# Attention: the heads' norm taken from the unnormalised result, with epsilon scaled by the squared sum of exponentials

## The chip, the cores and the metric

One core of one Trainium2 chip. The metric is the device time of one launch in microseconds (us); a kernel's time is the median of its runs. A difference of about 0.2% (7.6 us) is the least that a measurement of this kernel can tell from none.

## The reference, cut to what matters

The program is two layers of a diffusion backbone over 1024 latent tokens, with 256 context tokens that share the weights (in the second layer the context is only read). Each layer: a norm, an input projection, three parallel mixers (a long convolution, an mLSTM, differential attention), an output projection, and a mixture of 32 experts. The change lies in the attention alone:

```python
def diff_core(q, k, v, lam):
    s = jnp.einsum('bqhmd,bkhmd->bhmqk', q, k, preferred_element_type=jnp.float32) * (DA_HD ** -0.5)
    pr = jax.nn.softmax(s, axis=-1)
    a = pr[:, :, 0] - lam * pr[:, :, 1]
    return jnp.einsum('bhqk,bkhe->bqhe', a.astype(v.dtype), v)
...
    def finish(o):
        return (rmsnorm(o, p['da_subln_w']) * (1.0 - lam_init)).reshape(o.shape[0], o.shape[1], DA_V)
```

Four heads, each with two score maps (m = 0, 1) of 64 channels; the 128 output channels of a head are divided by their root mean square plus `NORM_EPS` = 1e-6. Write S0 and S1 for a row's sums of exponentials. The kernel never divides by S0: it forms u = e0 - (lam S0 / S1) e1 and U = u V, so that the head's output is U / S0, and the norm is (U / S0) / sqrt(mean(U^2) / S0^2 + eps). That equals U / sqrt(mean(U^2) + eps S0^2).

## The kernel before, in words

`attention` works through units. A unit is one head and 256 query tokens (16 per layer: four heads of four blocks); layer 0 has one more, the context tokens of all four heads. `x` = 0, 1 is the half of 128 query rows, `m` the score map. A pass of the loop runs three units at once, each one stage further: unit i gets its scores, maxima and exponentials, unit i-1 is transposed and rounded, unit i-2 is multiplied with V and its norm begun, and the last two steps of unit i-3's norm are done too. So a full pass is one with i from 3 to 15; the norm's last steps are missing in passes 0 to 2.

The order within a pass is written out by hand in `AT_ORDER` (L1240), and holds on PE, DVE, ACT and POOL (a manual schedule); SP's queue, which issues the loads of q, k and v and the stores, stands in an order that a planner set. The letters:

- `S`xm: six matmuls for one score tile `at_sc` (L1107, PE). There are two such tiles in PSUM.
- `M`xm: the negated row maximum (L1113, DVE). `E`xm: the exponentials and their sum (L1122, ACT).
- `C`x (`comb`): a reciprocal (L1130) and a product (L1131) that give c = -lam S0 / S1, then a reciprocal of S0 into `at_R` (L1132), all DVE on 128x1 tiles; on POOL the tile e1 is multiplied by c (L1134, 1280 columns) and added to e0 (L1138, 1280 columns, two inputs).
- `T`n: four transposes (L1150, PE); `U`n: the high part (L1161, ACT); `L`n: the low part (L1166, DVE).
- `O` and `Q` are steps of `out1`: `O` for unit i-2, `Q` for unit i-3. The first two `O` are 15 matmuls each with V (`at_av`, helper lines L68 to L70), the third copies and squares the result (ACT), the fourth sums the squares with ones (`at_st`, L1184, PE), the fifth does on DVE two products with `at_R` (L1188, L1189) and `mean + eps` (L186 in the helper `rstd`), and on POOL the power -1/2 (L188). In the next pass the first `Q` multiplies that by `at_R` (L1192, DVE), the second transposes it to a row vector `at_rb` (L1196, PE), the third scales the result (L1198, DVE) and stores it (L1199, SP).
- `W`: one sixteenth of the output projection's weights is loaded, and split on ACT (L1253) and POOL (L1254).

All of `at_t`, `at_av`, `at_st` and `at_rb` share two buffers in PSUM. While one of them holds the sums of `at_av`, the others take turns in the second: `at_rb` can be written only after `L1` has read its tile, and `T1` only after `L0`.

Of the kernel before, what the change touches and what calls it, by code (L numbers as in the profile page):

```python
# [8 lines left out]
F32 = mybir.dt.float32  # L9
# [3 lines left out]
OP = mybir.AluOpType  # L13
# [10 lines left out]
EPS = 1e-6  # L24
# [5 lines left out]
class Kern:  # L30
# [332 lines left out]
    def fft1(self, z, W, G, gD, pool, ps):  # L363
# [5 lines left out]
        for c in range(4):  # L369
            zn = [self.hsplit(pool, x(c + 1)) for x in z] if c < 3 else None  # L370
            S = pool.tile([128, 2, 2, 256], F32, name="f_s", bufs=2)
            for ri in range(2):
                p = ps.tile([128, 512], F32, name="f_p", tag="mm")
                for n, (w, x) in enumerate(zip(W, zz)):
                    self.mm3(p, [w[:, h, ri, :] for h in range(2)], x, start=(n == 0), stop=(n == len(W) - 1))
                nc.scalar.copy(S[:, ri].rearrange("p a b -> p (a b)"), p)
                self.qa.dma_start(rows[c, ri], S[:, ri].rearrange("p a b -> p (a b)"))
            zz = zn
# [246 lines left out]
    def hyena(self, l, cx, p, ps):  # L625
# [9 lines left out]
        for o in range(2):  # L635
# [28 lines left out]
            for c in range(4):  # L664
                S = p.tile([128, 2, 2, 256], F32, name="f_s", bufs=2)
                for ri in range(2):
# [369 lines left out]
    def attention(self, l, cx, p, pk, ps, psc, fill):  # L1036
        tc, nc, I = self.tc, self.nc, self.I
# [2 lines left out]
        N = len(pairs)  # L1040
        st = {}

        def prep(i):

            ctx = pairs[i] is None
            kt = lambda: pk.tile([128, 1280], F32R, name="at_k", bufs=6)
            vt = lambda: pk.tile([128, 10, 128], F32R, name="at_v", bufs=4)
            if ctx:
                kd = [[kt()[:, 0:1024].rearrange("p (h t) -> p h t", h=4) for y in range(2)] for m in range(2)]
                for m in range(2):  # L1050
                    for y in range(2):
                        for x in range(2):
                            nc.sync.dma_start(kd[m][y][64 * x:64 * x + 64].bitcast(F32),
                                              self.qkD[l][1, :, y, 64 * m:64 * m + 64, SEQ:].rearrange("h d t -> d h t"))
                v = [vt() for x in range(2)]
                for x in range(2):
                    for k in range(2):
                        nc.sync.dma_start(v[x][:, k:8:2, :].bitcast(F32),
                                          self.vD[l][x, SEQ + k * 128:SEQ + (k + 1) * 128, :]
                                          .rearrange("p (h e) -> p h e", h=4))  # L1060
                q = [kt()[:, 0:1024].rearrange("p (m h t) -> p m h t", m=2, h=4) for _ in range(2)]
                for qi in range(2):
                    for m in range(2):
                        c = SEQ + qi * 128
                        for y in range(2):
                            nc.sync.dma_start(q[qi][64 * y:64 * y + 64, m].bitcast(F32),
                                              self.qkD[l][0, :, y, 64 * m:64 * m + 64, c:c + 128]
                                              .rearrange("h d t -> d h t"))
            else:
                h, qb = pairs[i]  # L1070
                q = pk.tile([128, 2, 256], F32R, name="at_q", bufs=2)
                for y in range(2):
                    nc.sync.dma_start(q[64 * y:64 * y + 64].bitcast(F32), self.qkD[l][0, h, y, :, qb * 256:(qb + 1) * 256]
                                      .rearrange("(m d) t -> d m t", m=2))
                if qb == 0:
                    kd = [[kt() for y in range(2)] for m in range(2)]
                    for m in range(2):
                        for y in range(2):
                            for x in range(2):
                                nc.sync.dma_start(kd[m][y][64 * x:64 * x + 64, :].bitcast(F32),  # L1080
                                                  self.qkD[l][1, h, y, 64 * m:64 * m + 64])
                    v = [vt() for x in range(2)]
                    for x in range(2):
                        nc.sync.dma_start(v[x].bitcast(F32), self.vD[l][x].rearrange("(k p) e -> p k e", p=128)
                                          [:, :, h * 128:(h + 1) * 128])
                    st["kv"] = kd, v
                kd, v = st["kv"]
            nh = 4 if ctx else 1
            st[i] = dict(ctx=ctx, kd=kd, v=v, q=q, nh=nh, nk=8 if ctx else 10, E=[[None, None], [None, None]],
                         sc=[[None, None], [None, None]], t={},  # L1090
                         R=p.tile([128, 4, 2], F32, name="at_R", bufs=4),
                         S=[p.tile([128, 5, 4], F32, name=f"at_S{x}", bufs=2) for x in range(2)])

        def smm(i, x, m):
            u = st[i]
            w = u["nk"] * 128
            sc = u["sc"][x][m] = psc.tile([128, 1280], F32, name="at_sc", bufs=2)
            if u["ctx"]:
                for h in range(4):
                    for y in range(2):  # L1100
                        nc.tensor.matmul(sc[:, h * 256:(h + 1) * 256], u["q"][x][:, m, h, :], u["kd"][m][y][:, h, :],
                                         start=(y == 0), stop=(y == 1))
            else:
                for c in range(0, w, 512):
                    n = min(512, w - c)
                    for y in range(2):
                        nc.tensor.matmul(sc[:, c:c + n], u["q"][:, m, x * 128:(x + 1) * 128],  # L1107
                                         u["kd"][m][y][:, c:c + n], start=(y == 0), stop=(y == 1))

        def smx(i, x, m):  # L1110
            u = st[i]
            w, sc = u["nk"] * 128, u["sc"][x][m]
            nc.vector.tensor_reduce(u["S"][x][:, m, 0:u["nh"]], sc[:, 0:w].rearrange("p (h t) -> p h t", h=u["nh"]),  # L1113
                                    axis=AX.X, op=OP.max, negate=True)

        def sexp(i, x, m):
            u = st[i]
            w, S, g = u["nk"] * 128, u["S"][x], u["nk"] * 128 // u["nh"]
            e = u["E"][x][m] = p.tile([128, 1280], F32, name=f"at_e{m}", bufs=2 if m else 4)[:, 0:w]
            for h in range(u["nh"]):  # L1120
                cs = slice(h * g, (h + 1) * g)
                nc.scalar.activation(e[:, cs], u["sc"][x][m][:, cs], AF.Exp, bias=S[:, m, h:h + 1],  # L1122
                                     accum_out=S[:, 2 + m, h:h + 1])

        def comb(i, x):

            u = st[i]
            S, E, n = u["S"][x], u["E"][x], u["nh"]
            c = S[:, 4, 0:n]
            nc.vector.reciprocal(c, S[:, 3, 0:n])  # L1130
            nc.vector.scalar_tensor_tensor(c, S[:, 2, 0:n], nlam, c, op0=OP.mult, op1=OP.mult)  # L1131
            nc.vector.reciprocal(u["R"][:, 0:n, x], S[:, 2, 0:n])  # L1132
            if n == 1:
                nc.gpsimd.tensor_scalar(E[1], E[1], c, 1.0, op0=OP.mult, op1=OP.mult)  # L1134
            else:
                e = E[1].rearrange("p (h t) -> p h t", h=n)
                nc.gpsimd.tensor_tensor(e, e, c.unsqueeze(2).to_broadcast([128, n, 256]), op=OP.mult)
            nc.gpsimd.tensor_tensor(E[0], E[0], E[1], op=OP.add)  # L1138
# [29 lines left out]
        def out1(u, h, k0, nk):  # L1168
            o = ps.tile([128, 512], F32, name="at_av", tag="mm")
# [11 lines left out]
            R = u["R"][:, h if u["ctx"] else 0, :]  # L1181
            o = ps.tile([128, 512], F32, name="at_st", tag="mm")
# [1 line left out]
                nc.tensor.matmul(o[:, x:x + 1], sq[:, x * 128:(x + 1) * 128], self.ones[:, 0:1],  # L1184
                                 start=True, stop=True)
            yield
            t = p.tile([128, 2], F32, name="at_ms", bufs=2)
            nc.vector.tensor_tensor(t, o[:, 0:2], R, op=OP.mult)  # L1188
            nc.vector.tensor_tensor(t, t, R, op=OP.mult)  # L1189
            r = self.rstd(p, t, 2, 1.0 / 128)  # L1190
            yield
            nc.vector.tensor_tensor(R, r, R, op=OP.mult)  # L1192
            yield
            o = ps.tile([128, 512], F32, name="at_rb", tag="mm")
            for x in range(2):
                nc.tensor.transpose(o[:, x * 128:(x + 1) * 128], R[:, x:x + 1].to_broadcast([128, 128]), self.ident)  # L1196
            yield
            nc.vector.scalar_tensor_tensor(ob, ob, sub, o[:, 0:256], op0=OP.mult, op1=OP.mult)  # L1198
            nc.sync.dma_start(self.yTD[l][4 + h, :, u["qb"] * 256:(u["qb"] + 1) * 256], ob)  # L1199
# [7 lines left out]
        with tc.manual_schedule(engines={E_.PE, E_.DVE, E_.Activation, E_.Pool}):  # L1207
            for i in range(N + 3):
                prev, cur = cur, None
                if 0 <= i - 2 < N:  # L1210
                    u = st[i - 2]
# [20 lines left out]
            if cx:  # L1232
                for a in range(0, 4, 2):
# [3 lines left out]

    AT_ORDER = """S00 O M00 T0 S01 T1 U0 O L0 E00 Q Q U1 M01 S10 T2 L1 E01 T3 O Q S11 U2 C0 O T4 M10 U3 E10 L2 L3  # L1240
                  M11 U4 O E11 L4 C1 W"""


# [426 lines left out]
    S = 9  # L1670
# [194 lines left out]
    R = 5, 2, 2, 2, 1.5  # L1865
# [327 lines left out]
```

## Time and profile before

| | |
|---|---|
| median of 3 runs | 3781.49 us (3776.14 to 3783.82) |
| the profiled execution | 3769.79 us, its span 3768.0 us |
| busy share of the span | PE 85%, PE weight load 69%, DVE 73%, ACT 49%, POOL 46% |
| attention, layer 0 | from about 705 to 975 us of the span |
| attention, layer 1 | from about 2606 to 2832 us |
| mean granted PE clock | 0.927 of full speed |

PE is TensorE, PEld its weight loads, DVE VectorE, ACT ScalarE, POOL GpSimd, SP the queue that issues most transfers. Shares are means over stages with different limits, so the attention must be read by itself.

### The profile page before, as it was taken

The page shows a single profiled execution, that of the slowest core. Times are in us where ns is not written, and L with a number is a line of the kernel's source. Part 1 is how long each engine was busy: PE and PEld are TensorE (multiplying, and loading weights), DVE is VectorE, ACT ScalarE, POOL GpSimd, SP SyncE. Part 2 cuts the span into 40 slices and gives each one's busy share as a digit, 9 for nine tenths or more (in the row PEclk, how much of TensorE's full clock was granted, in tenths as well). Part 3 has the DMA queues.
Part 4 walks back from the last instruction along what each step waited for, and adds up shares of the span by engine and source line. Part 5 has one row for each costly group of instructions (what it writes and reads, how often), then busy time and mean ns, then how long its engine had stood idle before and what let it go on. Part 6 is the DMA issues. An engine that isn't in the chain of part 4 may idle for free. (4 is left out here: it accounts for less than half of the span.)

```text
span 3768.0 us, 49472 instructions
## 1 busy us (share of the span) xinstructions
PE 3211.9 (85%) x16750; PEld 2604.6 (69%) x16750; DVE 2751.6 (73%) x4303; ACT 1844.7 (49%) x2747; POOL 1714.6 (46%) x1293
## 2 busy tenths in 40 slices
PE   5999889787689889999996799987887988898893
PEld 2667778777577667777764777786776867676672
DVE  5444577588477798788776836875885788888887
ACT  3323333465332457577575324334663266666673
POOL 5001443376354345455553703343764355555555
PEclk7999999999799899999998899998998999999996
DMA  6889667443555679988886635766415588888885
GB/s 212 278 281 327 178 205 210 129 123 96 163 184 194 216 254 323 328 314 319 300 330 251 228 111 176 229 202 168 122 52 175 198 325 279 329 328 319 325 329 200
DMA packets 388513, 877.22 MB, mean 233 GB/s; under 512 B 60765, under 2 KB 244584, under 8 KB 332192
## 3 DMA queue, kind: packets, MB, share of 16 engines
q1 hardware_dynamic: 328945, 644.13, 51.4%
q10 hardware_dynamic: 25103, 145.74, 10.9%
q0 software_dynamic: 34208, 84.14, 6.9%
q8 instruction: 134, 2.20, 0.2%
q14 instruction: 123, 1.01, 0.1%
HBM read 750.32 MB, written 154.77 MB: 240 GB/s over the span
## 5 line engine op out<-in xcount | busy, mean ns | idle before, releaser
L1609 DVE TENSOR_TENSOR e_lo<-e_raw,e_hi 128x1024 fp32r<-128x1024 f32 x570 | 901.0, 1611 | 132.2 <-ACT e_hi L1608 124.9
L1608 ACT CAST e_hi<-e_raw 128x1024 fp32r<-128x1024 f32 x760 | 773.4, 1049 | 292.5 <-PE e_h L70 148.2
L1609 POOL TENSOR_TENSOR e_lo<-e_raw,e_hi 128x1024 fp32r<-128x1024 f32 x190 | 504.1, 2653 | 404.1 <-ACT e_hi L1608 352.7
L69 PE MATMUL e_h<-e_lo,e_xh 128*128 128x512 f32 x1024 | 422.8, 413 | 65.7 <-DVE e_lo L1609 53.0
L68 PE MATMUL e_h<-e_hi,e_xh 128*128 128x512 f32 x1024 | 413.3, 408 | 11.7 <-ACT e_hi L1608 8.9
L70 PE MATMUL e_h<-e_hi,e_xl 128*128 128x512 f32 x1024 | 405.6, 397 | 0.0
L69 PEld LDWEIGHTS e_h<-e_lo,e_xh 128*128 128x128 f32 x1024 | 195.5, 191 | 149.5 <-DVE e_lo L1609 83.6
L68 PE MATMUL p_u<-hT,u_w 128*128 128x512 f32 (+1 forms) x768 | 289.7, 377 | 3.6 <-ACT u_w L60 3.6
L69 PE MATMUL p_u<-hT,u_w 128*128 128x512 f32 (+1 forms) x768 | 287.3, 374 | 0.0
L70 PE MATMUL p_u<-hT,u_w 128*128 128x512 f32 (+1 forms) x768 | 285.6, 373 | 0.0
L68 PEld LDWEIGHTS e_h<-e_hi,e_xh 128*128 128x128 f32 x1024 | 195.2, 191 | 65.3 <-ACT e_hi L1608 24.4
L1122 ACT ACTIVATE at_e<-at_sc,at_S 128x1280 f32<-128x1280 f32 (+1 forms) x144 | 177.7, 1238 | 105.3 <-DVE at_S L1113 97.1
L1107 PE MATMUL at_sc<-at_k,at_q 128*128 128x512 f32 (+1 forms) x768 | 193.9, 389 | 32.3 <-DMA at_k<-qkD 23.6
L70 PEld LDWEIGHTS e_h<-e_hi,e_xl 128*128 128x128 f32 x1024 | 195.4, 191 | 36.5 <-issue 0.5
L69 PE MATMUL e_y<-e_lo,e_hh 128*128 128x512 f32 x512 | 205.5, 403 | 17.3 <-DVE e_lo L1609 14.2
L1113 DVE TENSOR_REDUCE at_S<-at_sc 128x1 f32<-128x1280 f32 (+1 forms) x132 | 194.2, 1472 | 35.1 <-PE at_sc L1107 29.9
L70 PE MATMUL e_y<-e_hi,e_hl 128*128 128x512 f32 x512 | 199.7, 397 | 7.1 <-DVE e_hl L61 7.1
L1138 POOL TENSOR_TENSOR at_e<-at_e,at_e 128x1280 f32<-128x1280 f32 (+1 forms) x66 | 192.2, 2913 | 5.5
L1134 POOL TENSOR_SCALAR at_e<-at_e,at_S 128x1280 f32<-128x1280 f32 x64 | 85.7, 1339 | 236.1 <-DVE at_R L1132 175.3
L1107 PEld LDWEIGHTS at_sc<-at_k,at_q 128*128 128x128 f32 x768 | 143.9, 202 | 62.1 <-issue 23.9
L68 PE MATMUL e_y<-e_hi,e_hh 128*128 128x512 f32 x512 | 175.2, 411 | 10.5 <-ACT e_hi L1608 6.6
L68 PEld LDWEIGHTS p_u<-hT,u_w 128*128 128x128 f32 x768 | 148.1, 193 | 35.8 <-issue 7.9
(574 smaller groups left out, 8195.4 us busy)
## 6 DMA issues: line engine op xcount, KB each, us to landing
e_raw<-in_moe_w_dram SPq DMA_DIRECT2D x259, 1024.0 KB
e_raw<-in_moe_w_dram ACTq DMA_DIRECT2D x121, 1024.0 KB
adaw<-in_ada_w_dram SPq DMA_DIRECT2D x48, 1024.0 KB
at_k<-qkD SPq DMA_DIRECT2D x64, 320.0 KB
u_raw<-in_w_in_dram SPq DMA_DIRECT2D x36, 512.0 KB
cb_y<-yD SPq DMA_DIRECT2D x36, 512.0 KB
hW<-in_c_hw_dram POOLq DMA_DIRECT2D x32, 512.0 KB, 4.6
at_v<-vD SPq DMA_DIRECT2D x16, 640.0 KB
```

The source lines that it names most:

```text
L68: mm(out, L[0], R[0], start=start, stop=False)
L69: mm(out, L[0], R[1], start=False, stop=False)
L70: mm(out, L[1], R[0], start=False, stop=stop)
L1107: nc.tensor.matmul(sc[:, c:c + n], u["q"][:, m, x * 128:(x + 1) * 128], u["kd"][m][y][:, c:c + n], start=(y == 0), stop=(y == 1))
L1113: nc.vector.tensor_reduce(u["S"][x][:, m, 0:u["nh"]], sc[:, 0:w].rearrange("p (h t) -> p h t", h=u["nh"]), axis=AX.X, op=OP.max, negate=True)
L1122: nc.scalar.activation(e[:, cs], u["sc"][x][m][:, cs], AF.Exp, bias=S[:, m, h:h + 1], accum_out=S[:, 2 + m, h:h + 1])
L1134: nc.gpsimd.tensor_scalar(E[1], E[1], c, 1.0, op0=OP.mult, op1=OP.mult)
L1138: nc.gpsimd.tensor_tensor(E[0], E[0], E[1], op=OP.add)
L1608: self.nc.scalar.copy(hi, raw)
L1609: (self.nc.gpsimd if pool else self.nc.vector).tensor_tensor(lo, raw, hi.bitcast(F32), op=OP.subtract)
```

## The change

The sum S0 of both halves is kept in one tile `at_S` (128x2x5x4). `comb` no longer takes 1/S0: after the second half one instruction writes eps S0^2 for both halves into `at_R`. In the norm one instruction forms mean(U^2) + eps S0^2, the power -1/2 follows on POOL, and its result goes to the transposes as it is. The step of `out1` that multiplied by `at_R` is gone, and one `Q` of `AT_ORDER` with it. (The loop over columns in `smm` is rewritten with the same bounds; a name there is set and not used.)

```diff
@@ prep
-                         S=[p.tile([128, 5, 4], F32, name=f"at_S{x}", bufs=2) for x in range(2)])
+                         S=p.tile([128, 2, 5, 4], F32, name="at_S", bufs=2))
@@ comb
             nc.vector.reciprocal(c, S[:, 3, 0:n])
             nc.vector.scalar_tensor_tensor(c, S[:, 2, 0:n], nlam, c, op0=OP.mult, op1=OP.mult)
-            nc.vector.reciprocal(u["R"][:, 0:n, x], S[:, 2, 0:n])
+            if x == 1:
+                s = u["S"][:, :, 2, 0:n].rearrange("p x h -> p h x")
+                nc.vector.scalar_tensor_tensor(u["R"][:, 0:n, :], s, EPS, s, op0=OP.mult, op1=OP.mult)
@@ out1
-            t = p.tile([128, 2], F32, name="at_ms", bufs=2)
-            nc.vector.tensor_tensor(t, o[:, 0:2], R, op=OP.mult)
-            nc.vector.tensor_tensor(t, t, R, op=OP.mult)
-            r = self.rstd(p, t, 2, 1.0 / 128)
-            yield
-            nc.vector.tensor_tensor(R, r, R, op=OP.mult)
+            t = p.tile([128, 2], F32, name="at_ms", bufs=3)
+            nc.vector.scalar_tensor_tensor(t, o[:, 0:2], 1.0 / 128, R, op0=OP.mult, op1=OP.add)
+            r = p.tile([128, 2], F32, name="rs_r", bufs=3)
+            nc.gpsimd.tensor_tensor(r, t, self.nhalf.to_broadcast([128, 2]), op=OP.pow)
             yield
             o = ps.tile([128, 512], F32, name="at_rb", tag="mm")
             for x in range(2):
-                nc.tensor.transpose(o[:, x * 128:(x + 1) * 128], R[:, x:x + 1].to_broadcast([128, 128]), self.ident)
+                nc.tensor.transpose(o[:, x * 128:(x + 1) * 128], r[:, x:x + 1].to_broadcast([128, 128]), self.ident)
@@ AT_ORDER
-    AT_ORDER = """S00 O M00 T0 S01 T1 U0 O L0 E00 Q Q U1 M01 S10 T2 L1 E01 T3 O Q S11 U2 C0 O T4 M10 U3 E10 L2 L3
+    AT_ORDER = """S00 O M00 T0 S01 T1 U0 O L0 E00 Q U1 M01 S10 T2 L1 E01 T3 O Q S11 U2 C0 O T4 M10 U3 E10 L2 L3
```

How this stands on DVE is shown for one full pass in two pieces. The first is the start of a pass, from the second half's c of the pass ahead (`C1`) to `L1`; before:

```order
L1130 RECIPROCAL at_S_6510<-at_S_6510 128x1
L1131 SCALAR_TENSOR_TENSOR at_S_6510<-at_S_6510,at_nl 128x1
L1132 RECIPROCAL at_R<-at_S_6510 128x1
L1113 TENSOR_REDUCE at_S_6651<-at_sc 128x1
L1166 TENSOR_TENSOR at_A_6678<-at_t,at_A_6677 128x4x128
L1192 TENSOR_TENSOR at_R<-rs_r,at_R 128x2
L1113 TENSOR_REDUCE at_S_6651<-at_sc 128x1
L1166 TENSOR_TENSOR at_A_6678<-at_t,at_A_6677 128x4x128
```

and now, in the same place:

```order
L1131 RECIPROCAL at_S<-at_S 128x1
L1132 SCALAR_TENSOR_TENSOR at_S<-at_S,at_nl 128x1
L1135 SCALAR_TENSOR_TENSOR at_R<-at_S 128x2
L1114 TENSOR_REDUCE at_S<-at_sc 128x1
L1169 TENSOR_TENSOR at_A_6668<-at_t,at_A_6667 128x4x128
L1114 TENSOR_REDUCE at_S<-at_sc 128x1
L1169 TENSOR_TENSOR at_A_6668<-at_t,at_A_6667 128x4x128
```

The product into `at_R` between `L0` and `M01` is gone, and a product of `at_S` with itself stands where the reciprocal stood. The second piece is the norm's fifth step, between `M11` and `L4`; before:

```order
L1113 TENSOR_REDUCE at_S_6652<-at_sc 128x1
L1188 TENSOR_TENSOR at_ms<-at_st,at_R 128x2
L1189 TENSOR_TENSOR at_ms<-at_ms,at_R 128x2
L186 TENSOR_SCALAR rs_v<-at_ms 128x2
L1166 TENSOR_TENSOR at_A_6678<-at_t,at_A_6677 128x512
```

and now:

```order
L1114 TENSOR_REDUCE at_S<-at_sc 128x1
L1191 SCALAR_TENSOR_TENSOR at_ms<-at_st,at_R 128x2
L1169 TENSOR_TENSOR at_A_6668<-at_t,at_A_6667 128x512
```

Three instructions became one. After the first half's c (`C0`) the reciprocal into `at_R` is gone with nothing in its place. In the whole program DVE has 3253 rows for 3393; on PE the order is the same row for row, with the transposes of `at_rb` reading `rs_r` for `at_R`. Outside the attention a few neighbours on ACT, POOL and SP change places, in the output projection and the experts; the loads of k and q on SP stand as before.

## Rows read from the trace of the kernel before

**Rows 1.** Busy time by stretch: length, PE, PEld, DVE, ACT, POOL, granted clock, DMA, GB/s.

```profile
770.58:784.86 14.28, 11.78 (x82) 10.40 (x81) 12.64 (x22) 9.47 (x17) 10.48 (x6) 1.00 0.50 139
801.17:805.17 4.00, 2.42 (x19) 2.22 (x19) 4.00 (x4) 1.42 (x3) 3.73 (x2) 1.00 0.00 0
805.17:809.17 4.00, 3.42 (x16) 3.12 (x17) 2.69 (x6) 2.40 (x5) 1.85 (x2) 0.68 0.32 97
...
729.17:740.99 11.82, 11.23 (x79) 10.06 (x78) 10.56 (x21) 9.47 (x17) 10.52 (x6) 1.00 0.15 44
```

**Rows 2.** Timeline of DVE in a full pass: start, length in us, instruction.

```profile
777.66 0.48 DVE L1198 SCALAR_TENSOR_TENSOR at_o<-at_o,at_sub,at_rb 128x256 f32<-128x256 f32 x1 [0.53 <-PE at_rb L1196]
...
784.65 0.22 DVE L1131 SCALAR_TENSOR_TENSOR at_S<-at_S,at_nl 128x1 f32<-128x1 f32 x1
784.79 0.16 DVE L1132 RECIPROCAL at_R<-at_S 128x1 f32<-128x1 f32 x1
...
786.29 0.69 DVE L1166 TENSOR_TENSOR at_A<-at_t,at_A 128x512 fp32r<-128x512 f32 x1
786.90 2.51 DVE L1192 TENSOR_TENSOR at_R<-rs_r,at_R 128x2 f32<-128x2 f32 x1
789.33 1.48 DVE L1113 TENSOR_REDUCE at_S<-at_sc 128x1 f32<-128x1280 f32 x1
790.74 0.67 DVE L1166 TENSOR_TENSOR at_A<-at_t,at_A 128x512 fp32r<-128x512 f32 x1
...
792.55 0.22 DVE L1131 SCALAR_TENSOR_TENSOR at_S<-at_S,at_nl 128x1 f32<-128x1 f32 x1
```

**Rows 3.** Timeline of POOL in the same pass.

```profile
785.04 1.34 POOL L1134 TENSOR_SCALAR at_e<-at_e,at_S 128x1280 f32<-128x1280 f32 x1 [0.88 <-DVE at_R L1132]
786.47 2.93 POOL L1138 TENSOR_TENSOR at_e<-at_e,at_e 128x1280 f32<-128x1280 f32 x1
789.36 1.26 POOL L1254 TENSOR_TENSOR wo<-wo_raw,wo 128x512 fp32r<-128x512 f32 x1
```

**Rows 4.** Instructions that touch at_R: count, shortest, median and longest in ns.

```profile
L1192 DVE TENSOR_TENSOR at_R<-rs_r,at_R x36: 149/2514/2573, 743.0 to 2831.3; 128x2 f32<-128x2 f32 x36
```

**Rows 5.** Timeline of PE in the same pass.

```profile
785.34 1.40 PE L1107 MATMUL at_sc<-at_k,at_q 128*128 128x512 f32 x6
787.04 0.66 PE L1150 MATMUL at_t<-cst,at_e 128*128 128x128 f32 x4 [0.30 <-DVE at_A L1166]
...
789.14 0.28 PE L70 MATMUL at_av<-at_A,at_v 128*128 128x256 f32 x1
791.46 0.43 PE L1196 MATMUL at_rb<-cst,at_R 128*128 128x128 f32 x2 [2.05 <-DVE at_A L1166]
```

**Rows 6.** Timelines of DVE and POOL in pass 2, ahead of the first L1192.

```profile
733.66 1.29 POOL L1254 TENSOR_TENSOR wo<-wo_raw,wo 128x512 fp32r<-128x512 f32 x1
734.38 0.59 DVE L1131 SCALAR_TENSOR_TENSOR at_S<-at_S,at_nl 128x1 f32<-128x1 f32 x1
736.57 2.93 POOL L1138 TENSOR_TENSOR at_e<-at_e,at_e 128x1280 f32<-128x1280 f32 x1
738.95 0.14 DVE L1188 TENSOR_TENSOR at_ms<-at_st,at_R 128x2 f32<-128x2 f32 x1
```

**Rows 7.** Timelines of DVE and PE where a head ends and the next begins.

```profile
865.47 0.48 DVE L1198 SCALAR_TENSOR_TENSOR at_o<-at_o,at_sub,at_rb 128x256 f32<-128x256 f32 x1 [0.53 <-PE at_rb L1196]
...
875.56 1.17 PE L1107 MATMUL at_sc<-at_k,at_q 128*128 128x512 f32 x5 [1.93 <-DMA at_k<-qkD]
877.12 1.48 DVE L1113 TENSOR_REDUCE at_S<-at_sc 128x1 f32<-128x1280 f32 x1
```

**Rows 8.** Timeline of DVE: two L1192 in a row, with a lower PE clock between.

```profile
801.17 2.52 DVE L1192 TENSOR_TENSOR at_R<-rs_r,at_R 128x2 f32<-128x2 f32 x1
816.52 2.52 DVE L1192 TENSOR_TENSOR at_R<-rs_r,at_R 128x2 f32<-128x2 f32 x1
```

**Rows 9.** Timeline of DVE in the context unit's last norm step.

```profile
973.99 0.16 DVE L1192 TENSOR_TENSOR at_R<-rs_r,at_R 128x2 f32<-128x2 f32 x1 [1.71 <-POOL rs_r L188]
```

More of the change, by code (lines that the diff above doesn't have):

```diff
@@ L1096, in smm @@
             w = u["nk"] * 128
+            c0 = m * 1280
             sc = u["sc"][x][m] = psc.tile([128, 1280], F32, name="at_sc", bufs=2)
@@ L1103, in smm @@
             else:
-                for c in range(0, w, 512):
-                    n = min(512, w - c)
+                for c, n in ((0, 512), (512, 512), (1024, 256)):
                     for y in range(2):
@@ L1112, in smx @@
             w, sc = u["nk"] * 128, u["sc"][x][m]
-            nc.vector.tensor_reduce(u["S"][x][:, m, 0:u["nh"]], sc[:, 0:w].rearrange("p (h t) -> p h t", h=u["nh"]),
+            nc.vector.tensor_reduce(u["S"][:, x, m, 0:u["nh"]], sc[:, 0:w].rearrange("p (h t) -> p h t", h=u["nh"]),
                                     axis=AX.X, op=OP.max, negate=True)
@@ L1117, in sexp @@
             u = st[i]
-            w, S, g = u["nk"] * 128, u["S"][x], u["nk"] * 128 // u["nh"]
+            w, S, g = u["nk"] * 128, u["S"][:, x], u["nk"] * 128 // u["nh"]
             e = u["E"][x][m] = p.tile([128, 1280], F32, name=f"at_e{m}", bufs=2 if m else 4)[:, 0:w]
@@ L1127, in comb @@
             u = st[i]
-            S, E, n = u["S"][x], u["E"][x], u["nh"]
+            S, E, n = u["S"][:, x], u["E"][x], u["nh"]
             c = S[:, 4, 0:n]
```

## The prediction

> **What bounds the attention now.** I read the shares first, stretch by stretch; then DVE's timeline through one pass, since DVE is the busiest engine there beside PE; then POOL's and PE's over the same microseconds. A full pass, from one `M00` to the next, takes 14.28 us; DVE works 12.64 of it, PE 11.78, POOL 10.48, ACT 9.47 [rows 1]. Neither is full, so the question is what each waits for.
>
> DVE's timeline answers it. Of its 12.64 us one instruction of 128x2 elements takes 2.51: L1192, the product into `at_R` [rows 2]. Over both layers its 36 instances have a median of 2514 ns and a shortest of 149 [rows 4], so it does not work for 2.4 us, it is held. By what: it starts at 786.90 and ends at 789.41; POOL's sum over 1280 columns starts at 786.47 and ends at 789.40 [rows 2, 3]. The two ends agree to 0.01 us. L1192 reads both inputs from SBUF. So does L1131, and where POOL works in the same way L1131 takes 0.59 us for its usual 0.22, ending with POOL's L1254 (734.97 and 734.95) [rows 2, 6]. L1188 has one input in PSUM, and takes 0.14 in the midst of POOL's sum [rows 6]. So on these rows a DVE instruction with two inputs in SBUF waits out POOL's two-input instruction, and one with an input in PSUM does not.
>
> Who waits for L1192: DVE is in order, so `M01` begins at 789.33 and `L1` ends at 791.41 [rows 2]. `at_rb` needs the buffer that `L1` empties, and starts at 791.46, though the matmuls ahead of it on PE had issued their last at 789.14, about 0.11 before the next could go: PE stands still from 789.25, 2.21 us [rows 5]. Behind `at_rb` in PE's queue stand `S10` and all the rest of the pass.
>
> The trace holds a control. Pass 2 runs everything but the norm's last steps, and takes 11.82 us [rows 1].
>
> **The change part by part.** The sum is made against the profiled execution, 3769.79 us for a span of 3768.0; the median of the runs is 11.7 us (0.3%) above it, and I carry the difference over to the median.
>
> *L1192 goes.* DVE can start `M01` at 786.90 instead of 789.33, 2.43 us earlier, if its scores are there: `S01` ends at 786.74 [rows 5]. `L1` would end near 789.0, and then not `L1` but PE decides: `at_rb` at 789.25 in place of 791.46. Gain 2.21 us a pass. What is late next is PE itself. The power whose result `at_rb` now reads directly is computed between `C0`'s and `C1`'s work on POOL, a third of a pass before.
>
> *At `C1`* a product of `at_S` with itself takes the place of the reciprocal. Its kind cost 0.22 us in L1131, the reciprocal 0.16 [rows 2]: 0.06 lost ahead of `M00`. Bounds: nothing, and 0.4 if it is held as L1131 was in pass 2 [rows 6]. I take 0.06, since no POOL work is under way at that point in rows 3: L1134 starts only at 785.04. Net 2.15 us a pass, 12.13 in place of 14.28. The control agrees: 11.82 plus the slot of `at_rb` and the scaling behind it.
>
> *The other small instructions* of a pass (the reciprocal at `C0`, two of the three in the norm's fifth step) are some 0.1 to 0.2 us each. I take nothing for them in a full pass: after `C0` DVE waits for `S10`, and after `L4` for the exponentials of `E11`. If that cover is gone they are worth up to 0.4 a pass.
>
> *A wait that grows.* POOL's L1254 follows `C1`'s sum and ends at 790.62 [rows 3]. In the shorter pass `C0`'s L1131, 1.09 us behind `at_rb` (792.55 against 791.46 [rows 2, 5]), comes at 790.34 and is held until 790.62, as in pass 2. `M10`, queued behind it, needs `S10`, which ends about 1.6 us after `at_rb` starts, at 790.85. So it costs nothing; at worst 0.37 a pass (0.59 less 0.22).
>
> *Where a head begins* (passes 4, 8, 12) half of its keys arrive late. `S01` then resumes 10.09 us after the scaling L1198 of the pass ahead (875.56 against 865.47), while `M01` starts at 877.12, right behind the held L1192: today the wait costs nothing [rows 7]. In an ordinary pass `S01` starts 7.68 us after L1198 (785.34 against 777.66) [rows 2, 5]. So L1192 was the cover of that transfer. Its loads are issued behind the store that L1198 feeds, so they come earlier only as L1198 does. With L1192 gone, `M01` waits for the scores, to 876.73 plus a hand-over: 0.3 us gained. I take 0.25. Bounds 0 and the full 2.15.
>
> *The clock.* In pass 7 PE is granted 0.68 of full speed for some microseconds, a mean of its two levels of 1.2 and 2.4 GHz, right after a stretch in which it was busy for only 2.42 of 4 us [rows 1]. That pass takes 15.35 us (801.17 to 816.52) [rows 8], 1.07 more than an ordinary one. Four passes a layer are like it. With PE's gap before `at_rb` closed I expect most of the falls to be gone, but a gap stays at each head's start: 6 us of 8.6. Bounds 0 and 8.6.
>
> *Tails.* Behind the last pass the norms of the last units run with little else: pow, a wait of DVE (1.71 us in one step), L1192, the transposes [rows 9]. Three instructions of some 0.16 us leave each of about four steps in series in either layer, 0.5 us a step: 4 us, bounds 0 and 6.
>
> *Elsewhere* the order differs by a few exchanged neighbours: nothing, bounds 4 either way.
>
> The sum: passes 3 to 15 of both layers are 26; 20 ordinary ones at 2.15 give 43.0, 6 at a head's start 1.5, the clock 6.0, the tails 4.0. Together 54.5 us: 3769.79 becomes 3715.3, and the median **3727.0 us**.
>
> A rule that speaks against so much: the Trainium skill ("VectorE: DVE Perf Modes", section "Rules for kernel authors") says not to fuse chained VectorE operations for speed, but to lower their count. By that rule the gain would be the count: 140 instructions fewer at 0.16 us, an estimate of 22 us, and 3759 us. The rows decide for the larger sum, since what goes with L1192 is a hold of 2.4 us and not an operation.
>
> **The rivals.**
>
> *A. The new product into `at_R` is held instead.* It too reads two inputs from SBUF, and it stands just where POOL begins `C1`'s work. If POOL is first, DVE stands until L1134 ends at 786.38, and if the sum follows without letting go, until 789.40: from 784.79 that is 4.6 us, ahead of `M00`, in all 16 passes of either layer. 32 x 4.6 = 147 lost against 54.5 gained: about 3874 us. It decides at who starts first: the reciprocal that stands there now starts at 784.79, L1134 at 785.04 [rows 2, 3], and both hang on the same L1131, so DVE has 0.25 us in hand. Chance 0.04. The Trainium skill ("SBUF — State Buffer", section "Who interferes with whom") states this rule: a VectorE instruction with two SBUF inputs contends with a GpSimd instruction that reads SBUF, the first holds the shared ports for its whole length and the other blocks. The ends in rows 2, 3 and 6 agree with it.
>
> *B. The change doesn't take away the wait.* If L1192 really waited for the power's result, `at_rb`, which now reads it, would wait as long, and only the lower count is left: within 8 us, about 3778. Against it: the equal ends, and that L1192 has no idle time noted before it. Chance 0.04.
>
> *C. A part of the gain only.* The hold of L1131 at `C0` costs its 0.37 in every ordinary pass (7.4), and the clock falls as often as now (6): 3740. For it: pass 2 shows the hold; PE has gaps left. Chance 0.17.
>
> *D. More.* The keys' loads move forward with the rest, so the heads' starts gain fully too (11), and no clock falls are left (3): 3713. Against it is the place of the loads on SP. Chance 0.09.
>
> **How the numbers follow.** The forecast has 0.66; C and D lie beside it with the same sign. The low end is D, 3713, less part of the other terms' upper bounds: 3710. The high end is C, 3740, with the tails at nothing (4) and code elsewhere at its bound (4), 3748, and 2 for the runs' spread: 3750. Faster by over 0.2% is the forecast, C and D, 0.92; within 0.2% is B, 0.04; slower is A, 0.04.
>
> **What would show it.** Right: a pass of about 12.1 us; no instruction of 128x2 on DVE over 0.3 us in the full passes; `at_rb` directly behind the matmuls with V, or held by the keys in passes 4, 8 and 12; fewer stretches under full clock. A would show as a long product into `at_R` at `C1`; B as a wait of `at_rb` for the power; C as L1131 of 0.5 us with `M10` late behind it. The forecast is wrong if the attention's two stretches shorten by less than 30 us together, or if the time appears again behind them.

## The result, and the profile after

The changed kernel takes 3718.65 us (median of 4 runs, 3708.77 to 3733.01), against 3782.41 for the kernel before beside it: ratio 0.9843, 95% interval 0.9821 to 0.9866. On a second chip it took 3721.81 against 3774.24, ratio 0.9857 (0.9840 to 0.9873). The profiled execution took 3717.29 us, its span 3715.5, so between the two profiles 52.5 us went where 54.5 were forecast; the medians of the first chip lie 63.8 apart, those of the second 52.4.

The page of the kernel after, its first part (busy us, share of the span, instructions):

```profile
PE 3201.1 (86%) x16750; PEld 2597.1 (70%) x16750; DVE 2670.2 (72%) x4162; ACT 1843.9 (50%) x2747; POOL 1718.3 (46%) x1293
```

Busy time by stretch, after (columns as in rows 1). The first row is a full pass, from one `M00` to the next:

```profile
795.85:807.94 12.09, 11.63 (x82) 10.47 (x81) 10.20 (x19) 9.47 (x17) 10.47 (x6) 1.00 0.47 122
834.00:838.00 4.00, 1.98 (x15) 1.61 (x12) 2.32 (x3) 2.38 (x4) 3.92 (x2) 1.00 0.03 10
2641.00:2645.00 4.00, 2.00 (x14) 1.63 (x13) 2.33 (x3) 2.17 (x3) 3.92 (x2) 1.00 0.12 27
2645.00:2649.00 4.00, 4.00 (x23) 3.90 (x22) 2.09 (x3) 2.92 (x7) 1.55 (x2) 0.59 0.00 0
```

The pass fell from 14.28 us [rows 1] to 12.09. DVE's share of it fell from 12.64 to 10.20, 2.44 us; PE's work stayed at 11.6 to 11.8, and now fills 96% of the pass. The other three rows are spoken of further down.

DVE's timeline in that pass, after (L1135 is the new product into `at_R`, L1114 the maximum, L1169 the low part, L1199 the scaling):

```profile
795.64 0.22 DVE L1132 SCALAR_TENSOR_TENSOR at_S<-at_S,at_nl 128x1 f32<-128x1 f32 x1
795.77 0.15 DVE L1135 SCALAR_TENSOR_TENSOR at_R<-at_S 128x2 f32<-128x2 f32 x1
795.85 1.48 DVE L1114 TENSOR_REDUCE at_S<-at_sc 128x1 f32<-128x1280 f32 x1
797.30 0.69 DVE L1169 TENSOR_TENSOR at_A<-at_t,at_A 128x512 fp32r<-128x512 f32 x1
797.91 1.48 DVE L1114 TENSOR_REDUCE at_S<-at_sc 128x1 f32<-128x1280 f32 x1
...
800.74 0.48 DVE L1199 SCALAR_TENSOR_TENSOR at_o<-at_o,at_sub,at_rb 128x256 f32<-128x256 f32 x1 [0.69 <-PE at_rb L1197]
...
801.33 0.31 DVE L1132 SCALAR_TENSOR_TENSOR at_S<-at_S,at_nl 128x1 f32<-128x1 f32 x1
801.89 1.49 DVE L1114 TENSOR_REDUCE at_S<-at_sc 128x1 f32<-128x1280 f32 x1 [0.25 <-PE at_sc L1108]
```

`M01` (797.91) now follows `L0` directly, where L1192 stood for 2.51 us [rows 2]. On PE the last matmul with V and `at_rb` are 0.12 us apart; before, 2.32 [rows 5]:

```profile
800.20 0.28 PE L70 MATMUL at_av<-at_A,at_v 128*128 128x256 f32 x1
800.32 0.38 PE L1197 MATMUL at_rb<-cst,rs_r 128*128 128x128 f32 x2
```

All instructions that use `at_R` on DVE, after (count, shortest, median and longest in ns), to be read against rows 4:

```profile
L1191 DVE SCALAR_TENSOR_TENSOR at_ms<-at_st,at_R x36: 146/148/160, 742.4 to 2782.5; 128x2 f32<-128x2 f32 x36
L1135 DVE SCALAR_TENSOR_TENSOR at_R<-at_S x33: 151/154/160, 720.9 to 2768.6; 128x2 f32<-128x2 f32 x32, 128x8 f32<-128x8 f32 x1
```

No instance is held. POOL in the same pass:

```profile
797.45 2.93 POOL L1141 TENSOR_TENSOR at_e<-at_e,at_e 128x1280 f32<-128x1280 f32 x1
800.34 1.28 POOL L1255 TENSOR_TENSOR wo<-wo_raw,wo 128x512 fp32r<-128x512 f32 x1
```

Where the 52.5 us went, from the starts of the scaling (L1198 before, L1199 after), which comes once in each pass from 3 to 15 (a pass in the table is one from scaling to scaling); us over both layers:

| stretch | before | after | difference |
|---|---|---|---|
| first `M00` to the first scaling | 85.7 | 82.3 | -3.4 |
| 18 passes that begin no head | 261.3 | 224.0 | -37.4 |
| 6 passes at a head's start | 89.8 | 83.0 | -6.8 |
| last full pass to the last scaling | 76.1 | 70.2 | -5.9 |
| all outside the attention | 3255.1 | 3256.1 | +1.0 |

### The profile page after: what moved, and what is told of

Its sections match the earlier page's. It is cut to its first block, busy times and chain, and to the rows that moved or that the text cites. A ratio compares the mean times of both kernels' runs of the same rounds, so it can differ in the third digit from the quotient of the medians.

```text
span 3715.5 us, 49380 instructions
## 1 busy us (share of the span) xinstructions
PE 3201.1 (86%) x16750; PEld 2597.1 (70%) x16750; DVE 2670.2 (72%) x4162; ACT 1843.9 (50%) x2747; POOL 1718.3 (46%) x1293
## 5 line engine op out<-in xcount | busy, mean ns | idle before, releaser
L68 PE MATMUL e_h<-e_hi,e_xh 128*128 128x512 f32 x1024 | 413.9, 408 | 11.7 <-ACT e_hi L1609 8.9
L1114 DVE TENSOR_REDUCE at_S<-at_sc 128x1 f32<-128x1280 f32 (+1 forms) x132 | 194.8, 1476 | 44.0 <-PE at_sc L1108 38.6
L1137 POOL TENSOR_SCALAR at_e<-at_e,at_S 128x1280 f32<-128x1280 f32 x64 | 85.5, 1337 | 205.7 <-DVE at_S L1132 151.6
```

Of the source, the lines that this page charges most:

```text
L68: mm(out, L[0], R[0], start=start, stop=False)
L1114: nc.vector.tensor_reduce(u["S"][:, x, m, 0:u["nh"]], sc[:, 0:w].rearrange("p (h t) -> p h t", h=u["nh"]), axis=AX.X, op=OP.max, negate=True)
```

## The experiments

The sum "from first to last scaling" below is the part of the attention between these two marks, both layers: 427.2 us before, 377.1 after (378.5 in the repeat).

**Is L1192 held for its two tensor inputs?** The kernel before, with that one instruction rewritten:

```diff
-            nc.vector.tensor_tensor(R, r, R, op=OP.mult)
+            for x in range(2):
+                nc.vector.tensor_scalar(R[:, x:x + 1], r[:, x:x + 1], R[:, x:x + 1], 1.0, op0=OP.mult, op1=OP.mult)
```

> The kernel before, with the product into at_R (L1192) alone rewritten: two instructions of 128x1 that each read one tensor and take the other factor as a scalar per row, in the same place and with the same wait for the power's result. Theory of the hold (a DVE instruction with two tensor inputs in SBUF waits out POOL's two-input sum): each takes about 0.15 us instead of 2.5, the pass falls from 14.28 to 12.1 to 12.4 us, and the kernel gains 40 to 52 us against the kernel before (ratio 0.986 to 0.990), nearly all that the change gains. Theory of the count: one instruction more in each of 36 steps, no gain, 0 to 6 us lost. Theory that L1192 waits for the power: still 2.4 us from the start of the first of the two to the end of the second, no gain.

Measured: ratio to before 0.9865 (0.9844 to 0.9886), first to last scaling 382.6 us, most passes that begin no head 12.05 to 12.11. The instructions that took L1192's place, of all passes, then one pair and POOL's sum over the same time:

```profile
L1193 DVE TENSOR_SCALAR at_R<-rs_r,at_R x72: 202/204/214, 745.0 to 2784.7; 128x1 f32<-128x1 f32 x72
```

```profile
796.15 0.32 DVE L1193 TENSOR_SCALAR at_R<-rs_r,at_R 128x1 f32<-128x1 f32 x2
```

```profile
795.69 2.94 POOL L1138 TENSOR_TENSOR at_e<-at_e,at_e 128x1280 f32<-128x1280 f32 x1
```

Two instructions in the place of one, with the same operands and the same wait for the power, run through in the midst of POOL's sum. This edit alone, which adds 36 instructions, gives nearly the whole gain of the change. The theory of the count and that of the wait for the power fall. The trace of the kernel before has the same pair side by side: in pass 2, in the midst of POOL's sum (736.57 to 739.50), L1188 with an input in PSUM takes 0.14 us [rows 6], and L1189 right behind it, with two tensors in SBUF and the same 128x2, ends with the sum:

```profile
739.13 0.39 DVE L1189 TENSOR_TENSOR at_ms<-at_ms,at_R 128x2 f32<-128x2 f32 x1
```

**The product on POOL, off DVE.** The same kernel, with `nc.gpsimd.tensor_tensor(R, r, R, op=OP.mult)` right behind the power, and nothing in L1192's place.

> The kernel before, with the product into at_R done on POOL right behind the power, so that the result is ready a third of a pass before it is used; DVE's instruction L1192 is gone, the order of everything else as it was. Theory of the hold: passes of 12.1 to 12.4 us, 40 to 52 us faster than the kernel before; POOL's added instruction of some 0.7 us (the power of 128x2 took 0.71) lies in POOL's idle time. Theory of the count (36 instructions fewer on DVE at 0.16 us each): 6 us faster at most.

Measured: ratio 0.9906 (0.9890 to 0.9923); first to last scaling 381.6 us, about as in the run above (382.6), and most such passes 12.03 to 12.10. By its median, 38.1 us faster, it falls 2 short of the expected 40 to 52; in the attention of the profile it does not. POOL's product costs 0.2 us:

```profile
L1191 POOL TENSOR_TENSOR at_R<-rs_r,at_R x36: 196/197/208, 739.5 to 2776.0; 128x2 f32<-128x2 f32 x36
```

**The hold put back.** The changed kernel, with its new product moved to where L1192 stood; `N` does for unit i-1 what stood in `comb`:

```diff
-    AT_ORDER = """S00 O M00 T0 S01 T1 U0 O L0 E00 Q U1 M01 S10 T2 L1 E01 T3 O Q S11 U2 C0 O T4 M10 U3 E10 L2 L3
+    AT_ORDER = """S00 O M00 T0 S01 T1 U0 O L0 E00 N Q U1 M01 S10 T2 L1 E01 T3 O Q S11 U2 C0 O T4 M10 U3 E10 L2 L3
```

> The changed kernel, with its new product into at_R (eps times the squared sum) moved from behind the second half's c to the place where L1192 stood, between L0 and M01, one pass later; the number of instructions is that of the changed kernel. Theory of the hold: the moved product takes 2.4 to 2.5 us in passes 3 to 15, the pass is 14.2 to 14.3 us again, and the kernel is 43 to 55 us slower than the changed one, within 12 us of the kernel before (ratio to before 0.997 to 1.003). Theory of the count: as the changed kernel, ratio to before 0.983 to 0.986. Theory that L1192 waited for the power's result: the moved product does not read it, so also as the changed kernel.

Measured: ratio to before 1.0036 (1.0022 to 1.0050), just past the upper bound expected; first to last scaling 427.6 us, the 427.2 of before. The moved product in all passes, one instance, and POOL beside it:

```profile
L1145 DVE SCALAR_TENSOR_TENSOR at_R<-at_S x33: 151/2489/2640, 720.9 to 2832.8; 128x2 f32<-128x2 f32 x32, 128x8 f32<-128x8 f32 x1
```

```profile
794.04 2.48 DVE L1145 SCALAR_TENSOR_TENSOR at_R<-at_S 128x2 f32<-128x2 f32 x1
```

```profile
793.58 2.92 POOL L1138 TENSOR_TENSOR at_e<-at_e,at_e 128x1280 f32<-128x1280 f32 x1
```

It ends at 796.52, POOL's sum at 796.50. This instruction reads nothing that the power makes, so the hold has nothing to do with the power. The kernel has every part of the change and its lower count, and its time gains nothing: the lower count by itself shows only behind the last full pass, where this run takes 72.5 us for 76.1. Part of what it loses is that the moved product is held in passes 1 and 2 too, where L1192 had no work: the stretch ahead of the first scaling is 7.4 us longer than before over both layers (93.1 against 85.7).

**The place, or the two inputs?** The same place, but two `tensor_scalar` of 128x1, each with S0 as its one tensor and S0 again as the factor per row, in place of the product.

> As the run before (the product into at_R in L1192's old place, between L0 and M01), but as two instructions of 128x1 with one tensor input each and the other factor as a scalar per row. If the two tensor inputs are what is held: each takes about 0.15 us, and the kernel stays within 8 us of the changed kernel (ratio to before 0.983 to 0.987). If the place itself is what costs (any small DVE instruction there waits for POOL): as the run before, ratio to before 0.997 to 1.003.

Measured: ratio 0.9847 (0.9830 to 0.9863); first to last scaling 381.0 us. All of them, and one pair in the midst of POOL's sum, which began at 792.28 and lasted 2.93:

```profile
L1147 DVE TENSOR_SCALAR at_R<-at_S x64: 202/204/206, 718.1 to 2759.2; 128x1 f32<-128x1 f32 x64
```

```profile
792.74 0.33 DVE L1147 TENSOR_SCALAR at_R<-at_S 128x1 f32<-128x1 f32 x2
```

So it is not the place, but the second tensor input in SBUF. That the two instructions are also narrower (128x1 for 128x2) is not the reason: L1131 is 128x1 with two tensors in SBUF, and is held [rows 6]. The four runs settle where the gain came from.

**What is left above 12.1 us.** Of the 18 passes that begin no head, five stay longer (12.43 to 15.00). In the pass from 826.39 to 840.22 (13.83 us) the trace shows a wait that the kernel before does not have. SP, ACT, DVE and PE in turn, after:

```profile
829.09 0.37 SPq L1253 DMA_DIRECT2D wo_raw<-in_w_out_dram  x1
```

```profile
835.62 0.62 ACT L1254 CAST wo<-wo_raw 128x512 fp32r<-128x512 f32 x1 [2.47 <-DMA wo_raw<-in_w_out_dram]
```

```profile
836.75 0.69 DVE L1169 TENSOR_TENSOR at_A<-at_t,at_A 128x512 fp32r<-128x512 f32 x1 [1.68 <-ACT at_A L1164]
```

```profile
837.50 0.66 PE L1153 MATMUL at_t<-cst,at_e 128*128 128x128 f32 x4 [2.02 <-DVE at_A L1169]
```

ACT's cast of `wo_raw` stands ahead of `U0` and waits for a load that was issued behind those of v; `U0`, `L0` and `T1` are late behind it. The same happens from 2633.62 (15.00 us). There PE, after a stretch of 2.00 busy us in 4, is granted 0.59 of full speed, a mean of its two levels of 1.2 and 2.4 GHz: the last two of the rows by stretch above (the second row is the stretch from 834 in the first case).

How much of such a wait the pass pays can be read from ACT. In an ordinary pass ACT is idle for 0.77 us behind the cast anyway, until `T0`; four passes have the wait, the one from 826.39 and three more. First the ordinary pass, then these three:

```profile
796.68 0.59 ACT L1164 CAST at_A<-at_t 128x512 fp32r<-128x512 f32 x1 [0.77 <-PE at_t L1153]
784.08 0.62 ACT L1254 CAST wo<-wo_raw 128x512 fp32r<-128x512 f32 x1 [1.43 <-DMA wo_raw<-in_w_out_dram]
2642.83 0.62 ACT L1254 CAST wo<-wo_raw 128x512 fp32r<-128x512 f32 x1 [2.46 <-DMA wo_raw<-in_w_out_dram]
2694.92 0.62 ACT L1254 CAST wo<-wo_raw 128x512 fp32r<-128x512 f32 x1 [1.33 <-DMA wo_raw<-in_w_out_dram]
```

The waits less 0.77 are 0.66, 1.70, 1.69 and 0.56 us. In the three passes at full clock the excess over 12.10 is 0.65, 1.73 and 0.56. So the late load costs 4.6 us, and the 1.6 that are left of the excess go with the one fall of the clock, in the pass of 15.00 us (granted 0.90 over the pass) and the next of 12.43 (0.98).

Two edits were to remove the wait. First, the load issued by POOL right behind the instruction that empties the buffer:

```diff
-                raw = p.tile([128, 512], F32, name="wo_raw", bufs=1)
-                nc.sync.dma_start(raw, wv[:, k, cs])
+        def load(j, q):
+            raw = p.tile([128, 512], F32, name="wo_raw", bufs=1)
+            q.dma_start(raw, wv[:, j // 2, j % 2 * 512:(j % 2 + 1) * 512])
+            return raw
...
+            if j < 15:
+                raw = load(j + 1, nc.gpsimd)
             yield
```

> The changed kernel, with the loads of wo_raw (but the first) issued by POOL right behind the instruction that empties the buffer, in place of SP behind the store of the pass. Theory that the late wo_raw load makes the excess passes (13.83 us from 826.39 and 15.00 from 2633.62, in which ACT waits for wo_raw ahead of U0): the load has a whole pass, ACT's cast of wo_raw waits for no transfer any more, these two passes take 12.1 to 12.5 us, and the attention is 4 to 6 us shorter in the profile. Rival (POOL's issue, of unknown length, takes POOL over the 1.6 us that it has free in a pass of 12.1): every pass grows by up to 1 us, 20 to 26 us lost. Rival (the excess comes from the clock alone): the passes stay at 13 to 15 us with no wait of the cast.

Beside it ran the changed kernel again:

> The changed kernel itself, unchanged, beside the next three runs on the same chip: ratio to before as first measured, 0.982 to 0.987.

The repeat gave the ratio 0.9857 told above, and excess passes of 12.66, 13.51, 13.74 and 12.87 us. Measured with POOL's loads: 0.9865 (0.9843 to 0.9887), first to last scaling 383.4 us, 4.9 more than the repeat. The cast still waits in both layers; in layer 0 (us in total, times, longest):

```profile
ACT wo L1258 <- DMA wo_raw<-in_w_out_dram: 2.8, 2, 2.1
```

In one pass of each layer it waits 2.12 us, and that pass takes 13.45: again the wait less 0.77 over 12.10. In the other two of the four places the trace notes a wait of 0.39 us and none, and the passes take 12.08 and 12.10. There the edit did what it was to do. But the passes at a head's start take 14.21 to 15.66 us (mean 15.15, against 14.35 in the repeat), and four of the six ran at a granted clock of 0.89, where in the repeat one did; why it fell more often no run shows. Second, the cast and its low part moved behind `C0`:

```diff
-    AT_ORDER = """S00 O M00 T0 S01 T1 U0 O L0 E00 Q U1 M01 S10 T2 L1 E01 T3 O Q S11 U2 C0 O T4 M10 U3 E10 L2 L3
-                  M11 U4 O E11 L4 C1 W"""
+    AT_ORDER = """S00 O M00 T0 S01 T1 U0 O L0 E00 Q U1 M01 S10 T2 L1 E01 T3 O Q S11 U2 C0 W O T4 M10 U3 E10 L2 L3
+                  M11 U4 O E11 L4 C1"""
```

> The changed kernel, with W (the cast of wo_raw on ACT, its low part on POOL, and with them the next load) moved from the end of a pass to behind C0, so that the cast stands between U2 and U3 instead of ahead of the next pass's U0; on SP the load of wo_raw then comes ahead of the loads of v. Theory that the late wo_raw load makes the excess passes: the cast waits for no transfer in a full pass, no pass outside a head's start takes over 12.5 us (12.66, 13.51, 13.74 and 12.87 in the repeat of the changed kernel), and layer 0's attention takes 237 us for 239.7, layer 1's 218 for 220.7. Rival (POOL: the low part of 1.28 us now lies between C0's sum and the power, and pushes the power and C1's product back): the ordinary passes grow by 0.1 to 1 us, 3 to 26 us lost. Rival (the clock alone): the excess passes stay.

Measured: 0.9878 (0.9860 to 0.9895), first to last scaling 381.3 us. The ordinary pass grew to 12.36 us, as the rival said; the cast still waits, three times in either layer, now ahead of `U3`. Only a head's first pass got shorter (13.0 to 13.8). Both edits miss in time: the first brought the wait under 0.77 us in two passes of four, and no run did so in all, so the 4.6 us are a reading of the traces and not a measured gain.

**The heads' starts.** Half of the next head's keys issued by ACT, one load in each pass of the head before (a step `K` behind the third `O`).

> The changed kernel, with half of the next head's key loads (the four of the first score map) issued by ACT one in each pass of the head before, in the place of the pass where ACT waits for T2, in place of all eight by SP right ahead of the head. Theory that a head's start waits for keys because SP issues ten loads of 0.6 us each back to back (802.14 to 808.4): the four others then come 2.4 us earlier, S01 waits for no at_k, the six passes at a head's start take 12.1 to 12.4 us instead of a mean of 13.84, 8 to 10 us gained. Rival (the time is that of the transfer, or of the matmuls that free the buffers): 13.5 to 14 us as now, nothing gained. ACT's issues can cost up to 0.3 us in each of 24 passes, 7 us, if they last longer than its wait for T2.

Measured: 0.9891 (0.9871 to 0.9910), 10.6 us above the repeat of the changed kernel by the medians; the six passes took 14.98 to 18.65 us, and PE waits longer for keys than before:

```profile
803.16 2.05 PE L1119 MATMUL at_sc<-at_k,at_q 128*128 128x512 f32 x5 [3.42 <-DMA at_k<-qkD]
```

This doesn't test SP's issue rate, since the expectation has the order of the loads wrong. SP's loads and PE's wait in the changed kernel, then SP's loads in this run:

```profile
802.14 2.39 SPq L1081 DMA_DIRECT2D at_k<-qkD  x4
804.62 1.25 SPq L1074 DMA_DIRECT2D at_q<-qkD  x2
805.92 2.52 SPq L1081 DMA_DIRECT2D at_k<-qkD  x4
810.38 1.18 PE L1108 MATMUL at_sc<-at_k,at_q 128*128 128x512 f32 x5 [1.48 <-DMA at_k<-qkD]
```

```profile
791.94 2.69 SPq L1083 DMA_DIRECT2D at_k<-qkD  x4
```

In the changed kernel the keys of a head's first score map are loaded a whole head ahead, so `S00` waits for none. Of the eight loads only the first four are for the head that begins: the wait at 810.38 is for the semaphores of the third and fourth, issued at 803.34 and 803.94. The last four are for the head after. What the edit moved to ACT is these last four; the four that `S01` needs SP issues back to back in both kernels. In both the DMA engines are nearly full until the keys are there (busy share 0.92 and 1.02 in the two stretches of 4 us from 802 in the changed kernel, 1.01 and 0.89 in the two from 794 in this run). That fits the rival, the time of the transfer, but no run shows it.

**The same pair of instructions elsewhere.** In the experts DVE and POOL share the low parts of the weights (128x1024, both inputs in SBUF), three quarters and one quarter. POOL's are given back to DVE:

```diff
-    GP = (1, 2, 1), (1, 0, 1), (0, 0, 1)
+    GP = ()
```

> The changed kernel, with POOL's quarter of the experts' low parts (e_lo, 128x1024, both inputs in SBUF) given back to DVE: 760 on DVE and none on POOL. In the changed kernel DVE's 570 take a mean of 1.61 us (shortest 1.15) beside POOL's 190 of 2.68 (shortest 2.35), 918 us in all. Theory of the hold: alone, each takes 1.15 to 1.25 us, so 760 take 875 to 950 us, and DVE's busy time is the same within 40 us with a third more of them; the time of the kernel is within 15 us of the changed one. Theory without a hold (the longer ones are long for another reason, and stay so): 760 at 1.61 us, 1224 us, DVE over its whole span in the second layer's experts (731 busy of 850 us now), and the kernel 100 us slower or more.

Measured: 3629.66 us against 3774.24, ratio 0.9619 (0.9603 to 0.9635). The costliest groups of the changed kernel's repeat (busy us, mean ns, idle before and its releasers):

```profile
L1610 DVE TENSOR_TENSOR e_lo<-e_raw,e_hi 128x1024 fp32r<-128x1024 f32 x570 | 900.2, 1610 | 137.3 <-ACT e_hi L1609 135.2
L1610 POOL TENSOR_TENSOR e_lo<-e_raw,e_hi 128x1024 fp32r<-128x1024 f32 x190 | 504.7, 2656 | 405.3 <-ACT e_hi L1609 352.7 <-issue 33.4 <-DVE e_lo L1610 6.9
L69 PE MATMUL e_h<-e_lo,e_xh 128*128 128x512 f32 x1024 | 424.4, 414 | 64.7 <-DVE e_lo L1610 51.7 <-POOL e_lo L1610 12.2
```

and with DVE alone:

```profile
L1610 DVE TENSOR_TENSOR e_lo<-e_raw,e_hi 128x1024 fp32r<-128x1024 f32 x760 | 904.5, 1223 | 132.5 <-ACT e_hi L1609 128.6 <-DMA e_raw<-in_moe_w_dram 0.3
L69 PE MATMUL e_h<-e_lo,e_xh 128*128 128x512 f32 x1024 | 410.5, 401 | 13.7 <-DVE e_lo L1610 13.5
```

DVE does a third more of them in 904.5 us instead of 900.2: POOL's 505 us of work had relieved it of nothing. As to the hold, that is what was expected; as to the time it is a miss, since I expected the same time within 15 us and got 92 us less. What I left out is the order of arrival: a held piece comes late, and PE waits for it (51.7 us for DVE's pieces, now 13.5). Over all matmuls PE's waits for low parts fell from 79.4 to 22.7 us, about half of the 110.9 between the two profiles; PE's own busy time fell by 60, from 3213.0 to 3153.4, at a mean granted clock of 0.931 for 0.925. How the second half comes about was not followed.

The same edit on the kernel before:

> The kernel before, with POOL's quarter of the experts' low parts given back to DVE as in u8. Theory of the hold: what it gives there has nothing to do with the attention, so the same 85 to 100 us as on the changed kernel (ratio to before 0.973 to 0.978), while L1192 keeps its 2.5 us and the pass its 14.28. Rival (DVE gained room in the experts only with the changed kernel's order there): under 40 us, ratio over 0.989.

Measured: ratio 0.9748 (0.9730 to 0.9765), 94 us, with L1192 at a median of 2498 ns as ever. The gain is independent of the change. With both edits:

> The changed kernel with both edits: POOL's quarter of the experts' low parts back on DVE (u8) and W behind C0 (u9). If the two act in different stages they add: 0.9619 less what u9 gains, ratio to before 0.959 to 0.963.

Measured: 0.9641 (0.9625 to 0.9657), just above the expected range and not below the first edit alone: the moved `W` gains nothing. The version that beats both kernels is the change with `GP = ()`, at 0.9619.

## Why the prediction was right

The forecast case happened: a gain of 52.5 us between the profiles for a sum of 54.5, and 3718.65 us for 3727.0, inside the range. The profiled execution came 2.0 us above the forecast one (3715.3), the median 8.4 below the forecast median: I carried over the 11.7 us that lay between profile and median before, and after the change that distance was 1.4. That the sum of the profiles came so near is in part luck: it lacks a loss of 4.6 us, and the other terms together gave 2.5 more than forecast, the tails most.

| step | forecast | measured |
|---|---|---|
| L1192 goes, net in an ordinary pass | 2.15 x 18 between the marks = 38.7 | 2.18 x 18 = 39.3 (14.28 to 12.10) |
| a head's start, without the clock | 0.25 x 6 = 1.5 | 0.43 x 6 = 2.6 |
| the clock | 6.0 | 8.4 gone, 1.6 come new: 6.8 |
| ACT's wait for `wo_raw` | not in the sum | -4.6 |
| tails | 4.0 | 5.9 |
| passes 0 to 3, both layers | 4.3 (two ordinary ones) | 3.4 |
| elsewhere | 0 | -1.0 |

*L1192 goes:* right in size and in path, and the runs show the cause (the first, third and fourth experiment). That PE decides next is right: `at_rb` follows the matmuls with V.

*At `C1`:* the product took 0.15 us, not the 0.22 of L1131; its shortest bound, nothing, was the nearest. Rival A did not happen in any of 33 instances (longest 160 ns). That such a product is held where POOL has started first, the third experiment shows.

*A wait that grows:* as said. L1132 at 801.33 ends at 801.64, POOL's L1255 at 801.62; `M10` behind it still waits 0.25 us for PE.

*Where a head begins:* the direction was right; the repeat gave a mean of 14.35 us for these passes (14.08 without one of 15.70 at a granted clock of 0.89), the first profile 13.84, so of the 0.43 a pass 0.2 to 0.5 is spread.

*The clock:* right. Before, eight passes took 1.05 us more (15.33 for 14.28), at a granted clock of 0.89, and these are gone; one fall is left, in another place, and costs 1.6.

*What is late next* is the step that fell short. Five passes that begin no head are longer by 6.2 us together (0.65, 1.73, 2.90, 0.33 and 0.56 over 12.10), of which 4.6 are waits for `wo_raw`. The prediction asked what becomes late next on DVE and PE only, and so has this at nothing. In the shorter pass the load of `wo_raw` behind a head's v loads became late, and ACT waits for it; in the kernel before ACT never waits for it in these stretches.

*Rival B* (a wait for the power) would have had the first experiment show no gain. *C* happened in neither part: one fall of the clock is left and not eight, and the hold at `C0` costs a pass nothing. *D*'s loads did not move forward with the rest.

The Trainium skill's rule in "VectorE: DVE Perf Modes", section "Rules for kernel authors", was worth 22 us by the count, an estimate. The third experiment has that count, and its time is no better than before. What the Trainium skill states in "SBUF — State Buffer", section "Who interferes with whom", that a VectorE instruction with two SBUF inputs and a GpSimd instruction that reads SBUF shut each other out, agrees with all four runs on L1192 and with the experts.

## What to carry to other kernels

Compare each small instruction's median with its shortest instance: one that is mostly ten times its shortest works for a tenth of its time, and the end of something on another engine tells what holds it. Here a DVE instruction with two SBUF tensors and POOL's two-input work shut each other out, and a factor read as a scalar per row, an input in PSUM, or another moment frees it. Before work is shared out to POOL, compare DVE's mean with its shortest: POOL's quarter of the experts' pieces gave DVE no time at all and cost 92 us. And when a pass gets shorter, ask of every engine and queue, not of the busiest two alone, which wait was covered until now.

## What the runs showed that was not expected

A 128x2 product in SBUF costs DVE 2.5 us beside POOL's sum, and 0.32 as two instructions of 128x1 with a scalar per row. Sharing work between DVE and POOL can have no yield: 570 pieces at 1610 ns beside POOL, 760 at 1223 ns without. And POOL's own product of 128x2 took 0.197 us against 0.70 for its power of the same shape, so a small product can stand on POOL where DVE would be held. The clock did not fall each time: after 834 to 838 us, with PE busy for 1.98 of 4 us, 1.00 was granted in the next 4 us, after 2641 to 2645, with 2.00, it was 0.59; what tells the two apart no run shows. Whether POOL's product with one tensor input (L1137) holds DVE as its sum does was not tried. The reverse is in the traces: POOL's L653 has one tensor in SBUF, takes 0.47 to 0.49 us in three of its four instances before, and 0.99 in the fourth, where a DVE instruction with two tensors in SBUF had begun 0.30 us ahead of it:

```profile
478.58 0.69 DVE L61 TENSOR_TENSOR f_lo<-hy_z,f_hi 128x512 fp32r<-128x512 f32 x1
478.88 0.99 POOL L653 TENSOR_SCALAR h_kt<-h_kt,cst 128x256 f32<-128x256 f32 x1 [5.37 <-DMA qkD<-da_r]
```
